# Biases of the experts as three bfloat16 parts, and gather rows and activations stored in the order of the operands' columns

## The chip, the cores and the metric

The kernel runs on one core of a Trainium2 chip. A core has a matrix engine (TensorE, PE in the profile; its weight loads are listed apart as PEld), VectorE (DVE), ScalarE (ACT), GpSimd (POOL), SyncE (SP), which here issues nearly all DMAs, and 16 DMA engines that move data between HBM and the core's memory SBUF. Products land in PSUM, eight banks of 512 float32 columns by 128 partitions. The metric is the device time of one execution in microseconds, as the median of the runs.

## The reference, cut to what matters

One layer for 256 tokens of width 1024 in float32: a mixer (stick-breaking attention and a state-space scan, merged by gates), cross-attention into 256 memory tokens, and a mixture of 32 experts of which each token takes four. The change is in the last of them:

```python
def expert_block(args):
    xb, e = args
    g = jnp.minimum(xb @ w_e_gate[e] + b_e_gate[e], SWIGLU_LIMIT)
    u = jnp.clip(xb @ w_e_up[e] + b_e_up[e], -SWIGLU_LIMIT, SWIGLU_LIMIT)
    act = (u + 1.0) * g * jax.nn.sigmoid(SWIGLU_ALPHA * g)
    return act @ w_e_down[e] + b_e_down[e]
```

Each expert has three weight matrices of 1024 x 1024 float32, 4.194 MB each. All 32 are read once, 402.7 MB.

## The kernel before

*Mixer and cross-attention* (the first 530 us). Projection weights come in pieces of 1 MB and are split into a high and a low part in a shorter format of float32: ScalarE copies the high part (`w_h`, line 96), VectorE subtracts for the low part (`w_l`, line 97), and TensorE makes three products per pair (lines 241 to 244 and 257 to 259). Splits are made three pieces ahead of their products, in four buffers. A scheduler with a cost model orders the instructions of each engine here; where the code switches it off (`manual_schedule`) the order is that of the code.

*Expert stage* (from 530 us). Experts go in groups of four. For a group, `gather` (line 971, products at line 980) collects the tokens of each expert into columns: the rows `xh` and `xl` (high and low part of the normalised tokens) are the stationary operand, a selection matrix is the moving one, 32 products of 256 columns a group. A stationary operand takes every fourth column of a row, since the weights are loaded with the rows `4 p + k` of a matrix in partition `p`. `xl` is made by GpSimd (line 49 within `normal`). Per expert, `bias_of` (line 910) starts the two PSUM banks of gate and up with the biases: a product of a one-hot column with `bgu` in float32, four products of 512 columns into 64 partitions each (line 904). `matmul_cols` (line 947, products at line 951) adds the products of the tokens with the weight chunks; `swiglu` (line 955) forms the activation in `ut`; `act_t` (line 966) transposes it in four steps, again over every fourth column (line 968), into `aT`; then the down products, per pair of experts into the banks `y2`. `scatter` (line 990) adds a pair's result to the tokens.

*Weight chunks.* Each matrix comes in two chunks of 2.097 MB, 192 in all, issued by SyncE in the order of use (line 668; the last expert's down matrix in 16 parts at line 664). A ring of ten slots holds them (tile `mw`), and a slot is issued again when its last product is done. Three slots can be filled during the mixer, the other seven when its buffers are given back at about 504 to 526 us.

*Between the two halves* `overflow` (line 1058 on) handles experts with more than 64 tokens in a loop that may run no time at all. Ahead of and behind that loop all engines meet, and SyncE waits for its loads in flight.

*The end* (from line 1270): the last expert's down products in halves, sums into the tokens, the last normalisation and the output.

Of the kernel before, what the change touches and what calls it, by code (L numbers as in the profile page):

```python
# [17 lines left out]
NB = T // P  # L18
# [100 lines left out]
def body(nc, tc, a, out, dbg=None, stop=99):  # L119
# [7 lines left out]
    with es:  # L127
# [555 lines left out]
        brt = xa.tile([P, NE], F32, name="brt")  # L683
        memh = xa.tile([P, KT, T], F32R, name="memh")
# [39 lines left out]
        nc.gpsimd.tensor_copy(iop, iop_i)  # L724

# [170 lines left out]
        left = cst.tile([P, NB, NE + 4], F32, name="left")  # L896
# [5 lines left out]
        def bias(pg, w, hot4):  # L902
# [7 lines left out]
        def bias_of(pg, w, e):  # L910
            bias(pg, w, lambda r: ident[:, 32 * r + e:32 * r + e + 1].to_broadcast([P, CAP]))
# [50 lines left out]
        def fours(kt):  # L962

            return slice(512 * (kt // 4) + kt % 4, 512 * (kt // 4) + 512, 4)

        def act_t(ut, pa, aT):
# [91 lines left out]
        def overflow():  # L1058
# [17 lines left out]
            hot = mo.tile([P, NE], F32, name="o_hot")  # L1076
            tmp = mo.tile([P, NB, NE], F32, name="o_tmp")
            c2 = mo.tile([P, 2, NB], F32, name="o_col")
            hotp = mo.tile([P, 4], F32, name="o_hotp")
            ovi = mo.tile([P, 1], I32, name="o_i")  # L1080
            shf = mo.tile([P, 2, 15], F32, name="o_shf")
            q32 = mo.tile([P, 4], F32, name="o_q32")
            nc.vector.tensor_scalar(q32, iota[:, 0:4], 32.0, None, op0=ALU.mult)
            with tc.If(nv > 0), tc.For_i(0, nv, 1):
# [5 lines left out]
                nc.vector.tensor_scalar(hotp, q32, ec, iop, op0=ALU.add, op1=ALU.is_equal)  # L1090
# [19 lines left out]
                for w in range(2):  # L1110
                    bias(pg, w, lambda q: hotp[:, q:q + 1].to_broadcast([P, CAP]))
                dst = [[pg[0][0:64], pg[0][64:128]], [pg[1][0:64], pg[1][64:128]], [y2[0][0:64], y2[1][64:128]]]
                for w in range(3):
                    if w == 2:
                        swiglu(pg, gt, ut, st)
                        act_t(ut, pa, aT)
# [45 lines left out]
        for quad in range(NE // 4):  # L1162
# [18 lines left out]
            for pr in range(2):  # L1181
# [13 lines left out]
                for q in range(2):  # L1195
# [48 lines left out]
                    act_t(ut, pa, aT)  # L1244
# [117 lines left out]
```

## Time and profile before

| what | value |
|---|---|
| median of 3 runs | 1497.47 us (1496.65 to 1499.45) |
| profiled execution, own time | 1497.82 us |
| its span, first to last instruction | 1496.1 us, mean granted TensorE clock 0.983 |
| TensorE busy | 1413.6 us (94%) |
| VectorE, ScalarE, GpSimd busy | 635.6 (42%), 416.2 (28%), 16.8 us (1%) |
| read from HBM | 487.33 MB, 326 GB/s over the span |

The profile is of one execution. Busy time of TensorE comes from records whose ends are modelled, so a full engine is not one at its peak; the pace of equal instructions in a row (start to start) says more than their duration. The slices show the span in 40 parts of 37.4 us. A float32 product shows as two records of matmul.

### The profile page before, as it was taken

How to read it: one execution, taken by the hardware profiler on the slowest of the kernel's cores; microseconds unless marked ns; L12 is line 12 of the kernel's file. 1: busy time of each engine (PE TensorE's matmuls, PEld its weight loads, DVE VectorE, ACT ScalarE, POOL GpSimd, SP SyncE). 2: the span in 40 equal slices, each digit the busy share in tenths (PEclk: the TensorE clock that was granted, in tenths of full speed). 3: DMA queues.
4: the chain of work that ended last, by engine and by line, in shares of the span. 5: the costliest groups of instructions: out<-in, count | busy, mean ns of one | idle time of the engine just before them, and what ended most of it. 6: DMA issues, size and time to landing. Idle time of an engine off the chain costs nothing. (4 is left out here: it accounts for less than half of the span.)

```text
span 1496.1 us, 18742 instructions
## 1 busy us (share of the span) xinstructions
PE 1413.6 (94%) x7890; PEld 830.1 (55%) x7890; DVE 635.6 (42%) x1004; ACT 416.2 (28%) x656; POOL 16.8 (1%) x36
## 2 busy tenths in 40 slices
PE   7999998998999999999999999979999999999996
PEld 7988898997899853343343343324334334334333
DVE  7666579998777451621221221221222222222213
ACT  5666678885545310010000000001001001001010
POOL 1000000000000010000000000000000000000001
PEclk9999999999999999999999999999999999999998
DMA  7544445554854689979999999998999999999991
GB/s 243 170 169 169 141 141 184 184 170 144 327 206 141 267 348 428 428 332 402 427 427 427 426 427 426 427 426 373 427 426 427 427 426 427 427 426 427 427 399 48
DMA packets 76133, 489.65 MB, mean 327 GB/s; under 512 B 7379, under 2 KB 11979, under 8 KB 51727
## 3 DMA queue, kind: packets, MB, share of 16 engines
q1 hardware_dynamic: 75772, 488.16, 80.8%
q8 instruction: 63, 1.03, 0.3%
q10 hardware_dynamic: 274, 0.27, 0.1%
q14 instruction: 24, 0.19, 0.0%
HBM read 487.33 MB, written 1.08 MB: 326 GB/s over the span
## 5 line engine op out<-in xcount | busy, mean ns | idle before, releaser
L951 PE MATMUL ps_gu<-mw,xg 128*64 128x512 f32 x2048 | 462.0, 595 | 0.0
L951 PEld LDWEIGHTS ps_gu<-mw,xg 128*64 128x64 f32 x2048 | 147.4, 137 | 269.0 <-issue 262.4
L951 PE MATMUL ps_y<-mw,aT 128*64 128x512 f32 x992 | 222.2, 595 | 0.0
L97 DVE TENSOR_TENSOR w_l<-w_raw,w_h 128x1024 fp32r<-128x1024 f32 x145 | 175.4, 1215 | 88.2 <-ACT w_h L96 87.9
L96 ACT ACTIVATE w_h<-w_raw 128x1024 fp32r<-128x1024 f32 x145 | 152.8, 1057 | 116.6 <-PE ps_t L243 71.8
L241 PE MATMUL ps_t<-hTh,w_h 128*128 128x256 f32 x576 | 164.0, 286 | 2.0 <-DVE gx L331 2.0
L243 PE MATMUL ps_t<-hTl,w_h 128*128 128x256 f32 x576 | 164.0, 285 | 0.0
L244 PE MATMUL ps_t<-hTh,w_l 128*128 128x256 f32 x576 | 162.6, 284 | 0.3 <-DVE w_l L97 0.3
L951 PEld LDWEIGHTS ps_y<-mw,aT 128*64 128x64 f32 x992 | 71.3, 138 | 134.0 <-issue 133.4
L969 ACT ACTIVATE aT<-ps_x 128x512 f32<-128x512 f32 x32 | 19.1, 597 | 342.9 <-PE ps_x L968 342.8
L241 PEld LDWEIGHTS ps_t<-hTh,w_h 128*128 128x128 f32 x576 | 109.9, 191 | 3.3 <-issue 3.1
L243 PEld LDWEIGHTS ps_t<-hTl,w_h 128*128 128x128 f32 x576 | 110.1, 191 | 0.2 <-issue 0.2
L244 PEld LDWEIGHTS ps_t<-hTh,w_l 128*128 128x128 f32 x576 | 109.6, 191 | 0.5 <-DVE w_l L97 0.5
L958 DVE TENSOR_SCALAR ut<-ps_gu 128x512 f32<-128x512 f32 x32 | 22.1, 691 | 199.2 <-PE ps_gu L951 198.9
L904 PE MATMUL ps_gu<-bgu,ident 128*64 128x512 f32 x256 | 71.4, 624 | 24.2 <-DVE gt L956 9.4
L956 DVE TENSOR_SCALAR gt<-ps_gu 128x512 f32<-128x512 f32 x32 | 22.1, 690 | 146.3 <-PE ps_gu L951 146.3
L996 DVE SCALAR_TENSOR_TENSOR y<-ps_y,scl,y 128x512 fp32r<-128x512 f32 x30 | 22.5, 751 | 131.3 <-ACT y L995 128.0
L995 ACT ACTIVATE y<-ps_y,scl 128x512 fp32r<-128x512 f32 x30 | 19.0, 684 | 205.1 <-PE ps_y L951 160.5
L957 ACT ACTIVATE st<-gt 128x512 f32<-128x512 f32 x32 | 20.1, 629 | 179.0 <-DVE gt L956 179.0
L904 PEld LDWEIGHTS ps_gu<-bgu,ident 128*64 128x64 f32 x256 | 17.7, 140 | 66.4 <-issue 26.2
L988 ACT ACTIVATE xg<-ps_x,gb 128x256 f32<-128x256 f32 x32 | 18.1, 564 | 119.4 <-PE ps_x L980 119.4
L1003 DVE TENSOR_TENSOR h<-h,ps_x 128x512 f32<-128x512 f32 x60 | 38.6, 682 | 25.2 <-PE ps_x L1002 25.2
(354 smaller groups left out, 1853.4 us busy)
## 6 DMA issues: line engine op xcount, KB each, us to landing
mw<-in_w_e_gate SPq DMA_DIRECT2D x64, 2048.0 KB, 18.1
mw<-in_w_e_up SPq DMA_DIRECT2D x64, 2048.0 KB, 23.0
mw<-in_w_e_down SPq DMA_DIRECT2D x62, 2048.0 KB, 15.2
w_raw<-in_w_in SPq DMA_DIRECT2D x39, 1024.0 KB, 5.1
w_raw<-in_w_ssd SPq DMA_DIRECT2D x8, 1024.0 KB, 5.2
w_raw<-in_w_sb SPq DMA_DIRECT2D x4, 1024.0 KB, 5.0
csb<-csd SPq DMA_DIRECT2D x8, 512.0 KB, 6.6
w_raw<-in_w_mix_out SPq DMA_DIRECT2D x4, 1024.0 KB, 5.0
```

What stands on the lines that cost most here:

```text
L96: nc.scalar.activation(h, src, AF.Copy)
L97: nc.vector.tensor_tensor(l, src, h.bitcast(F32), op=ALU.subtract)
L241: nc.tensor.matmul(o, wh[:, k, s], xh[:, kt], start=first and j % 2 == 0, stop=False, skip_group_check=True)
L243: nc.tensor.matmul(o, wh[:, k, s], xl[:, kt], start=False, stop=False, skip_group_check=True)
L244: nc.tensor.matmul(o, wl[:, k, s], xh[:, kt], start=False, stop=last, skip_group_check=True)
L904: nc.tensor.matmul(pg[w][64 * i:64 * i + 64], hot4(2 * w + i), bgu, start=True, stop=False, skip_group_check=True)
L951: nc.tensor.matmul(dst[i], lhs(4 * c + k), chunk[:, k, 512 * i:512 * i + 512], start=first and c == 0 and k == 0, stop=c == 1 and k == 3, ...
L956: nc.vector.tensor_scalar(gt, pg[0], LIMIT, None, op0=ALU.min)
L957: nc.scalar.activation(st, gt, AF.Sigmoid, scale=1.702)
L958: nc.vector.tensor_scalar(ut, pg[1], -LIMIT, LIMIT, op0=ALU.max, op1=ALU.min)
L996: nc.vector.scalar_tensor_tensor(yl[r], y2[i][r], scl[r, i:i + 1], yh[r].bitcast(F32), op0=ALU.mult, op1=ALU.subtract)
L1003: nc.vector.tensor_tensor(h2[:, b, s], h2[:, b, s], ps, op=ALU.add)
```

## The change

The biases of gate and up are loaded three times, into partitions 0 to 31, 32 to 63 and 64 to 95 of `bgr`, and turned into three bfloat16 parts in `bgu` (the value, the rest, the rest of the rest) by copies on ScalarE and subtractions on VectorE. A bias product then takes 96 rows: `ident3` has a one in rows e, 32 + e and 64 + e of column e, so one product adds the three parts. There are still four products an expert.

The gather rows `xh` and `xl` are written in the order of columns in which the gather reads them, by reads that step over four (`fours`). The last product of SwiGLU does the same, and goes into `gt` instead of `ut`; the transposes then read 128 columns in a row. The overflow loop gets the same forms, and three small tiles are moved to make room.

```diff
-        bgu = cst.tile([P, 512], F32, name="bgu")
+        bgu = cst.tile([96, 4, 512], BF16, name="bgu")
         for w, n in enumerate(("b_e_gate", "b_e_up")):
-            for i in range(2):
-                q = 32 * (2 * w + i)
-                nc.sync.dma_start(bgu[q:q + 32], a[n][0][:, 512 * i:512 * i + 512])
+            for q in range(3):
+                nc.sync.dma_start(bgr[32 * q:32 * q + 32, 2 * w:2 * w + 2], a[n][0].rearrange("e (i f) -> e i f", i=2))
+        for w in range(2):
+            s = slice(2 * w, 2 * w + 2)
+            nc.scalar.activation(bgu[:, s], bgr[:, s], AF.Copy)
+            for q in (1, 2):
+                for r in [slice(32 * t, 32 * t + 32) for t in range(q, 3)]:
+                    nc.vector.tensor_tensor(bgr[r, s], bgr[r, s], bgu[r, s], op=ALU.subtract)
+                    nc.scalar.activation(bgu[r, s], bgr[r, s], AF.Copy)
+        ident3 = cst.tile([96, 32], BF16, name="ident3")
...
+        def fours(x, sorted=True):
+
+            return x.rearrange("q (k p) -> q k p", k=4) if sorted else x.rearrange("q (p k) -> q k p", k=4)
+
...
-                split(nc, xh[:, b, s], xl[:, b, s], h2[:, b, s], copy=copy, sub=nc.gpsimd)
+                split(nc, fours(xh[:, b, s]), fours(xl[:, b, s]), fours(h2[:, b, s], False), copy=copy, sub=nc.gpsimd)
...
-                nc.tensor.matmul(pg[w][64 * i:64 * i + 64], hot4(2 * w + i), bgu, start=True, stop=False,
-                                 skip_group_check=True)
+                nc.tensor.matmul(pg[w][64 * i:64 * i + 64], hot.to_broadcast([96, CAP]), bgu[:, 2 * w + i], start=True,
+                                 stop=False, skip_group_check=True)
...
-            nc.vector.tensor_tensor(ut, ut, st, op=ALU.mult)
+            nc.vector.tensor_tensor(fours(gt), fours(ut, False), fours(st, False), op=ALU.mult)
...
-                nc.tensor.transpose(pa[:, P * f:P * f + P], ut[:, fours(f)], ident)
+                nc.tensor.transpose(pa[:, P * f:P * f + P], gt[:, P * f:P * f + P], ident)
...
-                            nc.tensor.matmul(o, x[:, b, fours(kt + i)], sel[:, b], start=i == 0 and b == 0 and x is xh,
+                            nc.tensor.matmul(o, x[:, b, P * (kt + i):P * (kt + i) + P], sel[:, b], start=i == 0 and b == 0 and x is xh,
```

Three places of the new order of instructions follow. Line numbers of the changed kernel lie 2 to 20 higher.

On SyncE, among the last weight loads of the mixer (`w_raw`); `brt` is the router's bias:

```order
 L82 DMA w_raw<-in_w_in 128x4x512 x2
 L82 DMA w_raw<-in_w_ssd 128x4x512
-L741 DMA brt<-in_b_router 128x32
+L713 DMA bgr<-in_b_e_gate 32x1024 x3
+L713 DMA bgr<-in_b_e_up 32x1024 x3
+L757 DMA brt<-in_b_router 128x32
 L82 DMA w_raw<-in_w_ssd 128x4x512
 L82 DMA w_raw<-in_w_mix_out 128x4x512 x4
```

The bias loads, four of 64 KB near the start before, are six of 128 KB here and stand ahead of the last `w_ssd` piece.

On ScalarE at the same place (`sq` and `sh` belong to the scan's normalisation, `w_h` are high parts of projection weights):

```order
 L96 ACTIVATE w_h<-w_raw 128x1024
 L581 ACTIVATE sq<-y 128x1024
-L96 ACTIVATE w_h<-w_raw 128x1024 x2
+L716 ACTIVATE bgu<-bgr 96x1024
+L96 ACTIVATE w_h<-w_raw 128x1024
+L716 ACTIVATE bgu<-bgr 96x1024
+L96 ACTIVATE w_h<-w_raw 128x1024
+L720 ACTIVATE bgu<-bgr 32x1024 x2
 L586 ACTIVATE sq<-ps_ms,epst 128x256
+L96 ACTIVATE w_h<-w_raw 128x1024
 L587 ACTIVATE sq<-sq 128x256
+L720 ACTIVATE bgu<-bgr 32x1024 x2
```

Eight copies now stand between the copies of the weights, six on 32 partitions that each wait for a subtraction on VectorE. Those six subtractions stand between `w_l` rows in the same way.

On TensorE, from the first expert to the second; `ps_gu` are the banks of gate and up, before:

```order
L951 MATMUL ps_gu_5758<-mw,xg 64x512 x16
L904 MATMUL ps_gu_5933<-bgu,ident 64x512 x2
L904 MATMUL ps_gu_5934<-bgu,ident 64x512 x2
L951 MATMUL ps_gu_5933<-mw,xg 64x512 x13
L968 MATMUL ps_x<-ident,ut 128x128 x4
L951 MATMUL ps_gu_5933<-mw,xg 64x512 x3
L951 MATMUL ps_gu_5934<-mw,xg 64x512 x16
```

and in the changed kernel:

```order
L971 MATMUL ps_gu_5785<-mw,xg 64x512 x16
L924 LDWEIGHTS ident_4651
L924 MATMUL ps_gu_5960<-bgu,ident_4651 64x512
L924 LDWEIGHTS ident_4651
L924 MATMUL ps_gu_5960<-bgu,ident_4651 64x512
L924 LDWEIGHTS ident_4651
L924 MATMUL ps_gu_5961<-bgu,ident_4651 64x512
L924 LDWEIGHTS ident_4651
L924 MATMUL ps_gu_5961<-bgu,ident_4651 64x512
L971 MATMUL ps_gu_5960<-mw,xg 64x512 x16
L971 MATMUL ps_gu_5961<-mw,xg 64x512
L986 MATMUL ps_x<-ident,gt 128x128 x4
```

The place of the biases is the same; the transposes of the first expert come four products later. Through the rest of the stage the order of products stays within a few of what it was.

## Rows read from the trace of the kernel before

**Rows 1.** The page's 40 slices: granted clock, DMA busy, GB/s.
```profile
PEclk9999999999999999999999999999999999999998
DMA  7544445554854689979999999998999999999991
GB/s 243 170 169 169 141 141 184 184 170 144 327 206 141 267 348 428 428 332 402 427 427 427 426 427 426 427 426 373 427 426 427 427 426 427 427 426 427 427 399 48
```
**Rows 2.** Busy time by stretch: length, engines (instructions), granted clock, DMA share, GB/s.
```profile
1200.00:1300.00 100.00, 94.89 (x438) 38.56 (x436) 21.57 (x39) 7.80 (x13) 0.00 (x0) 0.98 1.01 427
```
**Rows 3.** Chain of waits: shares on the page, two pieces (start, us, what).
```profile
PE 30%; DVE 2%; ACT 0%; issue 0%; DVEq 0%
...
1128.94 4.02 PE ps_x L980 x16
...
1243.44 4.11 PE ps_x L980 x16
```
**Rows 4.** Waits of SyncE's queue: total us, times, longest.
```profile
SPq L668 <- PE ps_gu L951: 538.8, 116, 18.1
```
**Rows 5.** Busy time by stretches of 10 us, columns as in rows 2.
```profile
540.00:550.00 10.00, 10.00 (x44) 5.57 (x42) 3.84 (x8) 1.13 (x2) 0.00 (x0) 1.00 0.48 173
...
660.00:670.00 10.00, 10.00 (x42) 7.06 (x44) 2.12 (x4) 1.69 (x3) 0.00 (x0) 0.83 0.50 213
670.00:680.00 10.00, 10.00 (x46) 4.63 (x44) 1.22 (x3) 0.56 (x1) 0.00 (x0) 1.00 0.51 190
...
1020.00:1030.00 10.00, 10.00 (x45) 4.87 (x47) 1.76 (x4) 1.13 (x2) 0.00 (x0) 1.00 0.64 241
```
**Rows 6.** SyncE in order of time: start, us from first to last issue, count.
```profile
651.94 22.33 SPq L668 DMA_DIRECT2D mw<-in_w_e_down  x3
```
**Rows 7.** Chain of waits, pieces of the group from 1128.94.
```profile
1134.82 2.07 PE ps_x L980 x8
...
1151.28 0.86 PE ps_gu L904 x4
1152.14 3.43 PE ps_gu L951 x16
...
1156.43 0.68 PE ps_x L968 x4
```
**Rows 8.** TensorE in order of time: products with contiguous weights, two forms.
```profile
502.04 0.28 PE L791 MATMUL ps_xo<-pT,xvh 128*128 128x256 f32 x1
502.16 0.29 PE L791 MATMUL ps_xo<-pT,xvl 128*128 128x256 f32 x1
...
516.99 0.81 PE L854 MATMUL ps_tr<-ident,h 128*128 128x128 f32 x6
```
**Rows 9.** In order of time: first gather products, GpSimd's last low part.
```profile
534.78 0.83 PE L980 MATMUL ps_x<-sel,xh 128*128 128x256 f32 x2
...
537.68 1.27 POOL L49 TENSOR_TENSOR xl<-h,xh 128x512 fp32r<-128x512 f32 x1 [0.36 <-DVE xh L48]
```
**Rows 10.** Busy time in the mixer; the page's groups of the split.
```profile
360.00:370.00 10.00, 10.00 (x85) 9.95 (x84) 8.46 (x11) 5.39 (x7) 0.00 (x0) 1.00 0.41 129
370.00:380.00 10.00, 10.00 (x87) 10.00 (x86) 4.41 (x4) 7.04 (x10) 0.00 (x0) 1.00 0.58 206
...
L97 DVE TENSOR_TENSOR w_l<-w_raw,w_h 128x1024 fp32r<-128x1024 f32 x145 | 175.4, 1215 | 88.2 <-ACT w_h L96 87.9
L96 ACT ACTIVATE w_h<-w_raw 128x1024 fp32r<-128x1024 f32 x145 | 152.8, 1057 | 116.6 <-PE ps_t L243 71.8
```
**Rows 11.** The end: busy time by stretch, then two pieces of the chain.
```profile
1456.00:1462.00 6.00, 4.81 (x28) 2.10 (x26) 1.10 (x2) 1.19 (x2) 0.00 (x0) 1.00 0.86 275
1462.00:1468.00 6.00, 4.78 (x18) 2.02 (x20) 0.97 (x2) 0.60 (x1) 0.00 (x0) 0.72 0.02 5
...
1474.43 3.51 PE ps_y L1275 x32
...
1480.21 3.65 PE ps_y L1275 x32
```

More of the change, by code (lines that the diff above doesn't have):

```diff
@@ L683, in body @@
         brt = xa.tile([P, NE], F32, name="brt")
+        bgr = xa.tile([96, 4, 512], F32, name="bgr")
+        ge = xa.tile([P, 3], F32, name="ge")
         memh = xa.tile([P, KT, T], F32R, name="memh")
@@ L705, in body @@
         tap("h1", h1)
[L708 removed]
+        bgu = cst.tile([96, 4, 512], BF16, name="bgu")
         for w, n in enumerate(("b_e_gate", "b_e_up")):
[L710 to L712 removed]
+            for q in range(3):
[8 more added lines that the diff above has]
+        ident3 = cst.tile([96, 32], BF16, name="ident3")
+        nc.vector.tensor_tensor(ident3, ident[:96, 0:32], ident[:96, 32:64], op=ALU.add)
+        nc.vector.tensor_tensor(ident3, ident3, ident[:96, 64:96], op=ALU.add)
         wr = xt_p.tile([P, KT, NE], F32, name="wr")
@@ L724, in body @@
         nc.gpsimd.tensor_copy(iop, iop_i)
+        for t in range(3):
+            nc.vector.tensor_scalar(ge[:, t:t + 1], iop, 32.0 * (t + 1), -32.0, op0=ALU.is_ge, op1=ALU.mult)
+        for t in range(3):
+            nc.vector.tensor_tensor(iop, iop, ge[:, t:t + 1], op=ALU.add)
         rows2 = xt_p.tile([4, 512], F32, name="rows2")
@@ L895, in body @@
         nc.vector.tensor_copy(top[:, :, 0:TOPK], tv[:, :, 0:TOPK])
-        left = cst.tile([P, NB, NE + 4], F32, name="left")
+        left = mt.tile([P, NB, NE + 4], F32, tag="aT", name="left")
         for b in range(NB):
@@ L901, in body, with bias @@
         rows_bcast(g2[1], "ln2_g", 1)
-        def bias(pg, w, hot4):
+        def bias(pg, w, hot):
             for i in range(2):
-                nc.tensor.matmul(pg[w][64 * i:64 * i + 64], hot4(2 * w + i), bgu, start=True, stop=False,
-                                 skip_group_check=True)
+                nc.tensor.matmul(pg[w][64 * i:64 * i + 64], hot.to_broadcast([96, CAP]), bgu[:, 2 * w + i], start=True,
+                                 stop=False, skip_group_check=True)
         def bank_pair():
@@ L910, in bias_of @@
         def bias_of(pg, w, e):
-            bias(pg, w, lambda r: ident[:, 32 * r + e:32 * r + e + 1].to_broadcast([P, CAP]))
+            bias(pg, w, ident3[:, e:e + 1])
         pg0 = bank_pair()
@@ L959, in swiglu, with act_t @@
             nc.vector.scalar_tensor_tensor(ut, ut, 1.0, gt, op0=ALU.add, op1=ALU.mult)
-            nc.vector.tensor_tensor(ut, ut, st, op=ALU.mult)
-        def fours(kt):
-            return slice(512 * (kt // 4) + kt % 4, 512 * (kt // 4) + 512, 4)
-        def act_t(ut, pa, aT):
+            nc.vector.tensor_tensor(fours(gt), fours(ut, False), fours(st, False), op=ALU.mult)
+        def act_t(gt, pa, aT):
             for f in range(4):
-                nc.tensor.transpose(pa[:, P * f:P * f + P], ut[:, fours(f)], ident)
+                nc.tensor.transpose(pa[:, P * f:P * f + P], gt[:, P * f:P * f + P], ident)
             nc.scalar.activation(aT, pa.rearrange("p (f i c) -> p f i c", f=4, i=2), AF.Copy)
@@ L1075, in overflow @@
             pa = x_bank()
-            hot = mo.tile([P, NE], F32, name="o_hot")
-            tmp = mo.tile([P, NB, NE], F32, name="o_tmp")
+            hot = ut[:, 0:NE]
+            tmp = gt[:, 0:NB * NE].rearrange("p (b e) -> p b e", b=NB)
             c2 = mo.tile([P, 2, NB], F32, name="o_col")
-            hotp = mo.tile([P, 4], F32, name="o_hotp")
+            hotp = mo.tile([P, 1], BF16, name="o_hotp")
             ovi = mo.tile([P, 1], I32, name="o_i")
             shf = mo.tile([P, 2, 15], F32, name="o_shf")
-            q32 = mo.tile([P, 4], F32, name="o_q32")
-            nc.vector.tensor_scalar(q32, iota[:, 0:4], 32.0, None, op0=ALU.mult)
             with tc.If(nv > 0), tc.For_i(0, nv, 1):
@@ L1089, in overflow @@
                 nc.vector.tensor_scalar(hot, iota[:, :NE], ec, None, op0=ALU.is_equal)
-                nc.vector.tensor_scalar(hotp, q32, ec, iop, op0=ALU.add, op1=ALU.is_equal)
+                nc.vector.tensor_scalar(hotp, iop, ec, None, op0=ALU.is_equal)
                 for i, v in enumerate((posm, prb)):
@@ L1110, in overflow @@
                 for w in range(2):
-                    bias(pg, w, lambda q: hotp[:, q:q + 1].to_broadcast([P, CAP]))
+                    bias(pg, w, hotp[:96])
                 dst = [[pg[0][0:64], pg[0][64:128]], [pg[1][0:64], pg[1][64:128]], [y2[0][0:64], y2[1][64:128]]]
@@ L1115, in overflow @@
                         swiglu(pg, gt, ut, st)
-                        act_t(ut, pa, aT)
+                        act_t(gt, pa, aT)
                     for c in range(2):
@@ L1243, in body @@
                     aT = mt.tile([P, 4, 2, CAP], F32, tag=("aT", "st")[q], name="aT")
-                    act_t(ut, pa, aT)
+                    act_t(gt, pa, aT)
                     acts.append(aT)
```

## The prediction

> **What bounds the kernel now.** I read the page's slices first. From about 700 us on the line GB/s stands at 426 to 428 in almost every slice, with the line DMA at 9 or 8 [rows 1]; a stretch of 100 us inside it has a DMA share of 1.01 while TensorE is busy 94.89 us of 100 [rows 2]. Two resources are full at once. The chain of waits names only one of them: it runs through TensorE, PE 30% of the span against DVE 2%, and no piece of it is a wait for a weight chunk [rows 3]. The waits of the queue that issues the loads say the same, 538.8 us of waiting for the gate and up products to give a slot back [rows 4]. A reader who stops there takes the expert stage for bound by TensorE alone.
>
> The balance is read from one group of four experts. From the gather at 1128.94 to the next at 1243.44 TensorE took 114.5 us [rows 3]. The weights of four experts are 12 x 4.194 MB = 50.3 MB, and 50.3 MB at 427 GB/s is 117.9 us. So the loads are already slightly the slower of the two, and TensorE runs behind them by what the ten slots hold. Taking TensorE time out therefore moves the end only (a) where DMA stood still for want of a slot and (b) behind the last landing.
>
> For (a) four stretches of 10 us tell where DMA stood still [rows 5]. Against 427 GB/s, 540 to 550 lost (427-173)/427 x 10 = 5.9 us, and nearly another microsecond lies around it, 6.9 in all. 660 to 680 lost 5.0 + 5.6 = 10.6 us. 1020 to 1030 lost 4.4 us. In the second, SyncE's three issues from 651.94 stretch over 22.33 us, so the last went out at 674.27, after a slot that the first products of the second group gave back [rows 6]. For (b), DMA is 0.86 busy from 1456 to 1462 and idle after it, so the last weights landed at 1456 + 0.86 x 6 = 1461.2; TensorE was then behind, and its last down products ended only at 1480.21 + 3.65 = 1483.9 [rows 11].
>
> **The change part by part.**
> *Biases on TensorE.* An expert has four bias products, 512 columns each into 64 PSUM partitions. In the trace each float32 product is two records, and four records cost 0.86 us, so 1.72 us an expert [rows 7]. A record of that form paces at 3.43 / 16 = 0.214 us [rows 7]. The bfloat16 product makes one pass where the record makes two. No 512-column bfloat16 product is in the trace. If the two halves of the array still run side by side, four products cost 2 x 0.214 = 0.43 us; if they run one after the other, 4 x 0.214 = 0.86. I take 0.43, since the float32 pair already runs side by side. Saved: 1.29 us an expert, at least 0.86.
> *Gather rows in order.* The 32 products of a group cost 4.02 us for 16 and 2.07 for each further 8 [rows 3, 7], 8.2 us, 0.26 us each, behind weight loads that step over every fourth column. Products of the same size with contiguous weights start 0.12 us apart [rows 8], so 32 cost 3.8 us. Saved: 4.4 us a group; half of it if something besides the step paces them.
> *Transposes in order.* Four cost 0.68 us [rows 7]; six contiguous ones 0.81 us with the last one's tail in it [rows 8], 0.11 us apart, so four cost 0.44. Saved: 0.24 us an expert, at least nothing.
> Sum per group of four: 4 x 1.29 + 4.4 + 4 x 0.24 = 10.5 us, at least 4 x 0.86 + 2.2 = 5.6. TensorE then needs 104 us (at most 109) where the loads need 117.9. Over 32 experts TensorE gives up 84 us (at least 45), most of which becomes waiting for weights.
> *What comes back of it, (a).* The second standstill ends with the issue at 674.27. Until then TensorE saves five and a half experts' biases, 7.1 us, the two gathers, 6.8 (the first partly covered, below), and four transposes, 1.0: 14.9, of which I count 14 for waits that stay. To keep DMA fed the slot has to come 10.6 us earlier, and 2.4 more because the first standstill shrinks too. 14 covers 13.0 by a hair. I leave 1.5 us of it standing: 9.1 us gained; with the lower bound of 8 us saved, 5.6 of 13.0 stay uncovered and the gain is 5.0.
> At the first standstill the first slot comes back after the gather's fifth and sixth tiles, and these need the low parts from GpSimd, done at 537.68 + 1.27 = 538.95 [rows 9]. That cover keeps the gain to 2.4 us; 0 if GpSimd's reads, now with a step of four, cost it 2 us.
> The stretch at 1020 stays: before it SyncE waits at the branch for all its loads to land, whatever TensorE does.
> Last landing: 1461.2 - 9.1 - 2.4 = 1449.7.
> *(b), the end.* With TensorE waiting for weights, what is late after the last landing is the half of the last down products that uses them. Back from the landing: 22 us before it the last up chunk is in, then 3.4 us of products, 4 of SwiGLU and transposes, 9 of expert 30's down products and start of a sum, then 3.51 us for the first half of expert 31, about 1 of eviction, 1.25 of sums, and 3.65 for the second half [rows 11]. The chain ends 3 to 4 us after the landing, one clock dip included 5. From the end of the down products to the end of the span is 1496.1 - 1483.9 = 12.2 us as before. So landing + 16.
> *The mixer side.* Six subtractions of 1024 columns at 1.215 us are 7.3 us more on VectorE, eight copies at 1.057 are 8.5 more on ScalarE [rows 10], placed around 355 to 380. There VectorE idled 1.5 + 5.6 and ScalarE 4.6 + 3.0 us [rows 10], and TensorE was full. Queued behind a waiting bias copy are the splits of the projection weights, made three splits ahead, about 8 us of products. So most is hidden; without that cover it would be 8.5 us on the path of everything behind. The six bias loads stand before the next projection weights on SyncE, 0.77 MB or 1.8 us at 427 GB/s, where DMA was 0.41 busy. I take +1 us, bounds -2 and +8.
> *Moved reads.* VectorE, ScalarE and GpSimd now read with a step of four values in the split and in SwiGLU's last product. Nothing in the trace shows such a read on these engines; TensorE's weight load, 0.26 against 0.12 us, would double a 0.69 us operation. For 31 experts TensorE has other products to do meanwhile; for the last it costs up to 0.7, held in the range. The Trainium skill (SBUF — State Buffer, Door 1: The DMA port swizzle) says that an access crossing to a new 16-byte line pays a penalty, so that four float32 are as far as one may step for free; the gather's pace agrees, and by that rule the engines that read so now would pay, on a path that waits for weights anyway.
> Sum: 1449.7 + 1 + 16 = 1466.7 span; the profiled execution took 1.7 us beside its span and lay 0.35 above the median, so 1466.7 + 1.35 = **1468 us**.
>
> **The rivals.**
> *The standstill stays:* if the bias halves run one after the other or the gather keeps its pace, the slot at 674 comes too late and only the end is shortened: 1461.2 + 1 + 16 + 1.35 = 1479.5. For it: 14 against 13 leaves no room.
> *TensorE was the whole bound:* the chain read by itself gives 1497.5 - 84 = 1413, or 1452 with the lower saving. Against it: 117.9 us of loads a group at a rate that never leaves 428.
> *Nothing comes of it:* the mixer gives away 8 us, the rest is lost at new waits: 1495 to 1500.
> *The clock, and slower:* TensorE now waits for weights about once a chunk. In the 10 us at 660, after waits around the scatter, its granted clock was 0.83 [rows 5]: a third of them at 1.2 GHz instead of 2.4, 1.7 us lost. A group leaves 117.9 - 104 = 14 us for that, eight such dips. Beyond eight a group TensorE is the bound again; slower than before from about 8 + (29 + 3)/8/1.7 = 10 to 11 a group, for instance 13 a group, 1468 + 5 x 8 x 1.7 = 1536. Against it: a starved TensorE still has 104 of 118 us of dense products, and one that falls behind stops waiting. The Trainium skill (TensorE: Matmul & The Clock Gate, HAM oscillation — how this bites in real kernels) describes a kernel whose waits for DMA between bursts throttle it at every tile; by that rule this one could end at the 1536 too. In the slices of the expert stage the granted clock stands at 9 tenths or more [rows 1], so I give it little.
>
> **How the numbers follow.** Forecast, 1456 to 1474: 0.66. Standstill stays, 1474 to 1486: 0.17. TensorE alone or a faster DMA, below 1456: 0.06. Nothing: 0.05. Slower: 0.06. A measurement tells about 0.2%, 3 us, from no change. Faster 0.89, same 0.05, slower 0.06. The range takes the forecast's and most of the first rival's: 1457 to 1483.
>
> **What would show it.** After: slices of 427 GB/s from 560 on except near 1015; TensorE busy some 84 us less in all, idle before the products on weights and released by their DMA; the chain naming those loads; the last landing near 1450 and the end 16 us behind it; bias products at 0.43 us an expert and gather products 0.12 us apart. Wrong would be a standstill near 665 that stays, a mixer that ends more than 3 us later (the first gather, at 534.78 now [rows 9], marks it), or granted clocks of 0.5 between groups.

## The result, and the profile after

The changed kernel took **1474.38 us** (median of 4, 1472.75 to 1476.22) beside 1497.06 us for the kernel before, a ratio of 0.9846 with the interval 0.9829 to 0.9863. That is 22.7 us less. Forecast were 1468 us and 29 us less: the sign and the main mechanism held, the time lies in the range, and the gain is 6 us short of the forecast. The profiled execution has a span of 1474.5 us and a time of 1476.22, 1.8 us above the median.

The page's slices of the kernel after (granted clock, DMA share, GB/s), to be laid beside [rows 1]:

```profile
PEclk9999999999999999999999999999999999999998
DMA  7545355644675589999999999999999999999994
GB/s 239 172 161 181 122 168 172 200 145 154 237 288 171 203 351 422 427 426 397 428 426 428 428 426 427 429 426 376 429 427 428 428 427 427 427 428 428 427 428 164
```

From the seventeenth slice on, the loads stand at 427. Apart from the last, two slices are lower: 397 near 670 us, where [rows 1] had 332 and 402, and 376 near 1015, where they had 373. The first of the two shrank, the second did not. No slice of the stage but the last shows less than 9 tenths of the clock; stretches at half clock that are shorter than a slice come below.

The same by stretches (columns as in [rows 2]); the first line answers [rows 2], the next five [rows 5], the last the first two of [rows 11]:

```profile
1200.00:1300.00 100.00, 87.90 (x416) 34.54 (x418) 26.20 (x45) 8.46 (x14) 0.00 (x0) 0.98 1.01 427
540.00:550.00 10.00, 10.00 (x50) 4.24 (x48) 4.62 (x10) 1.32 (x3) 0.99 (x1) 0.94 0.46 154
660.00:670.00 10.00, 10.00 (x54) 4.38 (x52) 2.08 (x5) 1.13 (x2) 0.00 (x0) 1.00 0.80 311
670.00:680.00 10.00, 10.00 (x50) 4.29 (x46) 3.18 (x4) 0.63 (x1) 0.00 (x0) 1.00 1.01 429
1020.00:1030.00 10.00, 8.50 (x46) 3.34 (x44) 4.66 (x9) 0.60 (x1) 0.00 (x0) 1.00 0.87 341
1005.00:1030.00 25.00, 22.70 (x116) 9.07 (x114) 7.84 (x13) 1.82 (x3) 0.00 (x0) 1.00 0.86 352
1450.00:1455.00 5.00, 5.00 (x38) 2.52 (x36) 0.00 (x0) 0.00 (x0) 0.00 (x0) 1.00 0.44 138
```

In the 100 us from 1200 on, DMA is as full as before and TensorE has 87.9 us of work instead of 94.9. The standstill near 665 lost (427-311)/427 x 10 = 2.7 us instead of 10.6. The one near 545 did not shrink: 6.4 us in this stretch, 5.9 before. The one near 1020 now begins earlier, so it is read over 25 us: (427-352)/427 x 25 = 4.4 us, as before. The last landing, reckoned from the busy share as in the prediction, is at 1450 + 0.44 x 5 = 1452.2 instead of 1461.2, so 9.0 us earlier. From there to the end of the span are 22.3 us instead of 34.9, so 12.6 us less. The two together are the 21.6 us by which the span fell.

The page's chain of waits and the queue of SyncE (us in total, times, longest), which answer [rows 3] and [rows 4]:

```profile
DMA 19%; PE 12%; DVE 1%; issue 0%; ACT 0%; SPq 0%; DVEq 0%
DMA mw<-in_w_e_down 11%; DMA mw<-in_w_e_up 8%; PE ps_gu L971 7%; PE ps_y L971 3%; PE ps_x L998 1%; PE ps_y L1291 0%; PE ps_x L851 0%; PE ps_acc L1173 0%; PE ps_gu L924 0%; PE ps_x L1019 0%; DVE y L1014 0%; PE ps_x L986 0%; ACT y L1013 0%; DVE h L1021 0%; SPq L668 0%
```

```profile
SPq L668 <- PE ps_gu L971: 252.7, 69, 14.2
SPq L668 <- DMA mw<-in_w_e_down: 161.1, 39, 4.9
SPq L668 <- DMA mw<-in_w_e_gate: 130.9, 31, 5.4
SPq L668 <- DMA mw<-in_w_e_up: 118.1, 30, 5.0
```

The chain now runs through the weight loads, which no piece of it named before. Both chains reach back only to about 1000 us (1007.7 before, 984.3 here), where the engines meet between the two halves, so their shares tell of the last third of the span. SyncE waits for TensorE to give a slot back for 252.7 us instead of 538.8, and for loads that are still under way for 410 us.

The pieces of the chain in one group (start, us, what), beside [rows 7]:

```profile
1110.64 2.17 PE ps_x L998 x16
...
1114.68 1.14 PE ps_x L998 x8
...
1118.54 1.13 PE ps_x L998 x8
...
1129.26 0.22 PE ps_gu L924 x2
...
1133.13 0.58 PE ps_x L986 x4
...
1171.19 39.54 DMA mw<-in_w_e_down
```

Two bias products take 0.22 us, so four take 0.43, as forecast (1.72 before). The 32 gather products take 2.17 + 1.14 + 1.13 = 4.44 us (8.2 before, 3.8 forecast). Four transposes take 0.58 (0.68 before, 0.44 forecast). Half a group further on the chain leaves TensorE and follows a load.

### The profile page after: what moved, and what is told of

The parts are those of the page before. It is cut to its first block, busy times and chain, and to the rows that moved or that the text cites. A ratio compares the mean times of both kernels' runs of the same rounds, so it can differ in the third digit from the quotient of the medians.

```text
span 1474.5 us, 18501 instructions
## 1 busy us (share of the span) xinstructions
PE 1353.5 (92%) x7762; PEld 796.4 (54%) x7762; DVE 657.0 (45%) x1017; ACT 425.5 (29%) x664; POOL 17.8 (1%) x36
## 3 DMA queue, kind: packets, MB, share of 16 engines
HBM read 487.85 MB, written 1.08 MB: 332 GB/s over the span
## 5 line engine op out<-in xcount | busy, mean ns | idle before, releaser
L971 PE MATMUL ps_gu<-mw,xg 128*64 128x512 f32 x2048 | 467.2, 599 | 17.9 <-DMA mw<-in_w_e_up 11.7
L971 PE MATMUL ps_y<-mw,aT 128*64 128x512 f32 x992 | 228.9, 604 | 19.3 <-DMA mw<-in_w_e_down 19.3
L924 PE MATMUL ps_gu<-bgu,ident 96*64 96x512 bf16 x128 | 26.8, 394 | 22.3 <-DVE gt L977 12.4
L1019 PE MATMUL ps_x<-y,selT 128*128 128x512 f32 x60 | 25.0, 458 | 18.1 <-ACT y L1013 11.3
```

Source lines behind the costliest of these rows:

```text
L924: nc.tensor.matmul(pg[w][64 * i:64 * i + 64], hot.to_broadcast([96, CAP]), bgu[:, 2 * w + i], start=True, stop=False, skip_group_check=True)
L971: nc.tensor.matmul(dst[i], lhs(4 * c + k), chunk[:, k, 512 * i:512 * i + 512], start=first and c == 0 and k == 0, stop=c == 1 and k == 3, ...
L1019: nc.tensor.matmul(ps, selT[r, i, P * b:P * b + P], yh[r], start=True, stop=False)
```

## The experiments

My theory: the weight loads bound the expert stage, so TensorE time that is taken out counts only at the standstills of DMA and behind the last landing. The rival: TensorE is the bound, and every microsecond that it loses comes off the end. All ratios are to the kernel before, run beside each kernel (1496.9 to 1497.3 us).

**One half of the change each.** `order_alone` is the kernel before with the ordered storage:

```diff
-                split(nc, xh[:, b, s], xl[:, b, s], h2[:, b, s], copy=copy, sub=nc.gpsimd)
+                split(nc, fours(xh[:, b, s]), fours(xl[:, b, s]), fours(h2[:, b, s], False), copy=copy, sub=nc.gpsimd)
...
-            nc.vector.tensor_tensor(ut, ut, st, op=ALU.mult)
+            nc.vector.tensor_tensor(fours(gt), fours(ut, False), fours(st, False), op=ALU.mult)
...
(gather and transposes read contiguous columns, as in the change)
```

> The kernel before with only the ordered storage of gather rows and activations; float32 biases in one product as before, no splitting of biases in the mixer. Loads are the bound: a group's TensorE time falls by some 4 to 5 us (gather 8.2 to 4.45, transposes 0.68 to 0.58 an expert), the standstill near 665 shrinks by some 4 us, TensorE catches up with the loads and ends 24 to 27 us behind the last landing instead of 34.9: 1481 to 1487, 10 to 16 us faster than before; with the other half alone this adds up to more than 22.7. TensorE is the bound: about 35 us saved of about 75, so 10.5 of the 22.7 us: 1486.5, and the halves add up to 22.7. No mixer cost: the first gather at 534.8, not 535.7.

`bias_alone` is the changed kernel with these lines put back.

> The change without its second half: bfloat16 biases in three parts, but gather rows and activations stored and read as in the kernel before. Loads are the bound: TensorE saves 1.3 us an expert, of which only what comes ahead of the standstill near 665 counts (some 4 of the 7.7 us that the whole change took out of it) and what TensorE is behind the last landing (34.9 us before; it catches up with the loads in any case, so 24 to 26 stay). Less 1 us for the mixer: 1480 to 1485, that is 12 to 17 us faster than before. TensorE is the bound: the gain of 22.7 us splits as the saved TensorE time does, 31 x 1.3 = 40 us of about 75: 12 us, 1485. The two theories are told apart only together with the other half: by the first, the two gains add up to more than 22.7 us, by the second to 22.7. Further: the standstill of 540 to 550 is as wide as in the kernel before if the clock and not GpSimd's stepped writes held it; with GpSimd at fault it shrinks by 1 us or more against the changed kernel.

Measured: `order_alone` 1481.74 us, 0.9892 (0.9877 to 0.9908); `bias_alone` 1480.89 us, 0.9898 (0.9883 to 0.9913). That is 15.1 and 16.0 us faster, 31.1 together, where the whole change gave 22.7. Each gain is known to about 2 us, so the 8 us between are clear of the noise. The gains do not add up, as the theory said and the rival did not. Stretches of `bias_alone`, then of `order_alone`:

```profile
655.00:685.00 30.00, 29.76 (x131) 15.84 (x131) 6.86 (x12) 2.88 (x5) 0.00 (x0) 1.00 0.75 305
...
1455.00:1460.00 5.00, 4.30 (x36) 2.38 (x32) 0.57 (x2) 0.84 (x2) 0.00 (x0) 1.00 0.09 29
```

```profile
655.00:685.00 30.00, 28.06 (x138) 13.07 (x137) 10.00 (x16) 4.15 (x7) 0.00 (x0) 1.00 0.83 345
...
1455.00:1460.00 5.00, 5.00 (x29) 2.01 (x30) 0.00 (x0) 0.00 (x0) 0.00 (x0) 1.00 0.39 127
```

Against 427 GB/s the standstill near 665 costs 8.6 and 5.8 us (10.5 before, 2.8 after, by the same sum). The last landing lies at 1455.5 and 1457.0, so 5.7 and 4.2 us earlier than before. The spans of 1477.4 and 1480.7 us then leave 21.9 and 23.7 us behind the landing. So either half alone brings the 34.9 us of the tail down to about what both bring (22.3): once TensorE needs less than the loads it catches up, and more saving adds nothing there. That common part is why the gains do not add.

**No biases at all.** The changed kernel without the bias products, the first weight product of a bank starting its sum:

```diff
-            bias(pg, w, ident3[:, e:e + 1])
+            return
...
-                                    ..., got[i], c, ks=ks)
+                                    ..., got[i], c, ks=ks, first=True)
```

> The changed kernel with the experts' gate and up biases left out of the expert stage altogether (the first weight product of a bank starts its sum). TensorE has 32 x 0.43 = 14 us less to do. Loads are the bound: 1472 to 1474, at most 2 us faster than the changed kernel (the part of 0.43 x 6 experts ahead of the standstill near 665, and 1 us of the tail). TensorE is the bound: 1474.4 - 13 = 1461.

Measured: 1476.45 us, 0.9866 (0.9851 to 0.9881). Taking a further 14 us of TensorE's work out gave nothing; if anything it took 2 us (within the spread of the runs). The rival's 1461 is excluded, but the time alone is not a clean test: the mean granted clock of the four runs is 0.972 to 0.977, against 0.983 to 0.987 in the changed kernel, so some of the 14 us went into products at half clock. What decides is where TensorE's time went. Its waits ahead of the weight products grew from 17.9 + 19.3 to 23.2 + 37.4 us, while DMA stayed full. The down products on the two pages (their idle time and what ended it are the last column), the changed kernel first, and 400 us of `no_bias`:

```profile
L971 PE MATMUL ps_y<-mw,aT 128*64 128x512 f32 x992 | 228.9, 604 | 19.3 <-DMA mw<-in_w_e_down 19.3
...
L971 PE MATMUL ps_y<-mw,aT 128*64 128x512 f32 x992 | 236.2, 618 | 37.4 <-DMA mw<-in_w_e_down 36.8
...
1030.00:1430.00 400.00, 350.05 (x1608) 127.22 (x1608) 94.24 (x155) 33.28 (x55) 0.00 (x0) 0.98 1.01 428
```

**Half the loads.** Both kernels, with every second chunk of weights left out once the first eleven are on their way:

```diff
                 w, e, c = plan[len(got)]
+                if c == 1 and len(got) > nslots and (w < 2 or e < NE - 1):
+                    got.append(got[-1])
+                    continue
```

> The kernel before with half of the weight loads of the expert stage left out: from the sixth expert pair's turn of the ten slots on, the second chunk of each matrix is not loaded and the first is used twice (the last expert's down matrix is loaded whole). TensorE's work is unchanged, DMA carries half. Theory (before, TensorE ran at its own pace behind full loads and hardly waited for them): 1490 to 1497. If the loads had held it back already: 1480 or less.

> The changed kernel with the same half of the weight loads left out. Theory (TensorE has 60 to 80 us less to do, and the loads alone keep the changed kernel from showing it): 60 to 80 us under the kernel before with half loads, 1415 to 1435, TensorE without waits for weights. Rival (TensorE's own work or the engines that feed it set the time of the changed kernel): about 1470.

Measured: 1477.71 us, 0.9870 (0.9855 to 0.9885), and 1401.16 us, 0.9357 (0.9343 to 0.9372). The busy line of the page, of the kernel before with half loads and of the changed one:

```profile
PE 1424.2 (96%) x7890; PEld 844.7 (57%) x7890; DVE 634.5 (43%) x1004; ACT 415.8 (28%) x656; POOL 16.8 (1%) x36
```

```profile
PE 1346.9 (96%) x7762; PEld 818.7 (58%) x7762; DVE 656.2 (47%) x1017; ACT 425.6 (30%) x664; POOL 17.8 (1%) x36
```

This is the change without its cover. It takes 1477.7 - 1401.2 = 76.5 us out of TensorE, and TensorE's busy time falls by as much, 77.3. With all loads it shows 22.7 of them, and the changed kernel takes 73 us more than with half of them.

Of the two expectations for the kernel before, the time of the second came: it got 19.3 us faster with half the loads, not 0 to 7. But that does not show that the loads had held it back. With half the loads the scheduler also laid the products in another order, in which bias products stand among weight products. The bias products on the two pages, before with all loads and with half:

```profile
L904 PE MATMUL ps_gu<-bgu,ident 128*64 128x512 f32 x256 | 71.4, 624 | 24.2 <-DVE gt L956 9.4
...
L907 PE MATMUL ps_gu<-bgu,ident 128*64 128x512 f32 x256 | 84.2, 619 | 5.2 <-PEq L1087 4.5
```

TensorE's idle time ahead of them, most of it for a bank that VectorE was still reading, fell from 24.2 to 5.2 us, and ahead of the scatter's first products from 19.9 to 12.5. Ahead of the weight products it was 0.0 in both. So in the kernel before TensorE never waited for a weight chunk, and the 19.3 us are not shown to be the loads'; the new order is enough to explain them. The 73 us hold some of the same: ahead of the changed kernel's bias products the idle time is 22.3 us, and 1.5 with half the loads. The 76.5 us between the two half-load kernels stand, since the busy time falls by as much.

**The tail.** Behind the last landing 22.3 us passed, not 16. TensorE in order of time at the end of the changed kernel (start, us, engine, line, count; in brackets its wait and what ended it):

```profile
1428.08 3.23 PE L851 MATMUL ps_x<-rows_a,ident 96*128 96x128 f32 x24
1431.23 7.09 PE L971 MATMUL ps_gu<-mw,xg 128*64 128x512 f32 x32
1441.09 0.63 PE L986 MATMUL ps_x<-ident,gt 128*128 128x128 f32 x4 [2.77 <-DVE gt L982]
...
1458.21 3.67 PE L1291 MATMUL ps_y<-mw,aT 128*64 128x256 f32 x32
```

TensorE has no wait for weights here. The two last up chunks lie ready and are used back to back, because 24 of the 32 transposes that spread the last layer norm's rows stand ahead of them. `early_rows` moves these to the seventh group:

```diff
             e0 = 4 * quad
             fetch(6 * e0 + nslots)
+            if quad == 6:
+                gb = last_rows()
...
-                        gb = last_rows()
```

> The changed kernel with one move: the 32 transposes that spread the last layer norm's gain and bias (4.3 us of TensorE) are issued at the start of the seventh group of experts, where TensorE waits for weights, and not with the last expert. My explanation of the tail (TensorE, not the loads, is late in the last 60 us, because these products, the slots' and the sums' starts all stand there): the last landing stays near 1452, the end comes 4 us earlier, about 1470. Rival (the last landing sets the tail, slowed to some 340 GB/s by the last expert's loads in pieces): no change, 1474.

Measured: 1471.42 us, 0.9821 (0.9808 to 0.9835), 3.0 us less than the changed kernel (the two intervals just overlap; the trace shows where the 3 us come from). The same place there, and its last landing:

```profile
1427.53 3.65 PE L971 MATMUL ps_gu<-mw,xg 128*64 128x512 f32 x16 [0.40 <-DMA mw<-in_w_e_up]
1432.43 3.65 PE L971 MATMUL ps_gu<-mw,xg 128*64 128x512 f32 x16 [1.25 <-DMA mw<-in_w_e_up]
```

```profile
1450.00:1455.00 5.00, 4.30 (x37) 2.63 (x33) 0.84 (x2) 0.84 (x2) 0.00 (x0) 1.00 0.49 158
```

Now TensorE waits for both up chunks, which is what my forecast had assumed. The landing stays (1452.5) and the tail is 1472.2 - 1452.5 = 19.7 us, as the explanation had it and not its rival, a tail set by the last landing alone. `late_acc` also moves the start of the first sums behind the last up products:

```diff
-                    if e == NE - 1:
-                        acc = [start_acc(0)]
                     for w in range(2) if e > 0 else ():
                         for c in range(2):
                             project(w, c)
+                    if e == NE - 1:
+                        acc = [start_acc(0)]
```

> The changed kernel with the layer norm's rows moved to the seventh group and the start of the first block's sums moved behind the last up products, without the repeated bias products. If the repeated products gave nothing: 1470.5, as fill_late_acc, with 6.8 us at half clock at the first gather and 18 us from the last landing to the end. If they gave 1 us or more: 1471.5.

Measured: 1470.43 us, 0.9822 (0.9806 to 0.9838). TensorE there:

```profile
1430.63 3.65 PE L971 MATMUL ps_gu<-mw,xg 128*64 128x512 f32 x16 [1.25 <-DMA mw<-in_w_e_up]
1434.22 1.98 PE L1173 MATMUL ps_acc<-h,ident 128*128 128x512 f32 x4
1436.98 0.66 PE L986 MATMUL ps_x<-ident,gt 128*128 128x128 f32 x4 [0.78 <-DVE gt L982]
1437.56 3.65 PE L971 MATMUL ps_y<-mw,aT 128*64 128x512 f32 x16
```

```profile
1450.00:1455.00 5.00, 4.30 (x34) 2.91 (x34) 2.36 (x6) 0.84 (x2) 0.00 (x0) 1.00 0.15 47
```

The sums' start fills the wait for SwiGLU, 2.68 us before, 0.78 left. The 16 down products behind it take 3.65 us at full clock instead of 5.31, and the tail is 1468.7 - 1450.8 = 17.9 us. Of the 6.3 us that I missed there, the layer norm's rows are 2.6, the sums and the clock 1.8. The 1.8 are read from the two traces; the times do not tell `late_acc` from `early_rows` (0.9822 and 0.9821). The remaining 1.9 are of the size of what the last up chunk brings, though no run tests it: it was in at 1430.6, 20.2 us ahead of the last landing, where I had worked with 22.

**The first gather and the clock.** The standstill near 545 did not shrink. The stretch around the first gather, of `order_alone` and of the changed kernel (the granted clock is the third number from the end):

```profile
525.00:545.00 20.00, 17.53 (x108) 12.17 (x107) 13.76 (x32) 4.98 (x7) 7.05 (x5) 0.91 0.86 358
```

```profile
525.00:545.00 20.00, 16.52 (x95) 11.63 (x94) 13.69 (x31) 4.93 (x7) 6.99 (x5) 0.83 0.80 333
```

Read in stretches of half a microsecond, 0.91 is 3.4 us of the 20 at 1.2 GHz instead of 2.4, and 0.83 is 6.8. The stretch stands at 0.91 in the three kernels with float32 biases (before, `order_alone`, `half_loads_before`). It stands at 0.83 in all nine with bfloat16 ones in which the wait was left as it is, `no_bias` among them. Ahead of the router's first position product TensorE was idle 1.86 us in the kernel before and 2.86 in the changed one: the same wait for the mask, with 0.41 us of bias products before it instead of 1.08. `fill_wait` repeats these products in that wait, in the version with the rows moved:

```diff
-        bias_of(pg0, 0, 0)
+        for _ in range(9):
+            bias_of(pg0, 0, 0)
```

> The changed kernel with the layer norm's rows moved (as in early_rows), and the first two bias products of the first expert repeated nine times, to the same sums, in the wait for the router's mask ahead of the first gather: 16 products more, some 2 us. In the four kernels with bfloat16 biases the clock was at half for 6.8 us at the first gather, in the two with float32 biases for 3.4 us. If the shorter bias products did this by leaving TensorE idle longer ahead of the gather, the stretch at half clock goes back to 3.4 us or away, the first slot comes back 8 us instead of 9.4 after the first gather's start, the standstill near 543 loses 1.4 us and the end comes 1 to 1.5 us earlier than in early_rows: 1470. If it is something else: 6.8 us at half clock and 1471.4 as there.

`fill_late_acc` is the same with the sums moved.

> As fill_wait, and the start of the first block's sums (two products of 512 columns, which each waited 0.8 us for a bank between weight products of the last expert) stands behind the last expert's up products instead, in the wait of 2.7 us for SwiGLU. If TensorE is late at the last weights by what stands ahead of them: the down products run at full clock and up to 2 us come off fill_wait. If the last up chunk's landing sets it (TensorE waited 1.25 us for it in early_rows) and the clock dips all the same: no change.

Measured: 1471.37 us, 0.9830 (0.9816 to 0.9843), and 1470.45 us, 0.9820 (0.9807 to 0.9834). The clock of the 20 us is 0.91 in `fill_wait`. Stretches of `fill_late_acc`, then of `late_acc`, which lacks the filling alone:

```profile
525.00:545.00 20.00, 17.15 (x115) 10.34 (x115) 14.10 (x34) 5.53 (x8) 7.03 (x5) 1.00 0.80 322
530.00:560.00 30.00, 27.40 (x149) 11.51 (x145) 16.62 (x37) 4.50 (x8) 5.42 (x4) 1.00 0.86 348
655.00:685.00 30.00, 30.00 (x149) 13.45 (x150) 6.72 (x11) 4.11 (x7) 0.00 (x0) 1.00 0.89 372
```

```profile
530.00:560.00 30.00, 26.93 (x129) 12.35 (x130) 17.18 (x37) 4.93 (x8) 5.88 (x4) 0.89 0.81 327
655.00:685.00 30.00, 29.89 (x148) 13.52 (x150) 7.38 (x13) 4.11 (x7) 0.00 (x0) 1.00 0.92 382
```

So it is the idle time that lengthens the stretch at half clock, and filling it shortens it or takes it away: two profiles against nine. Up to the last expert the two run the same instructions, so 0.91 against 1.00 is a difference between executions. At full clock the standstill near 545 loses (427-348)/427 x 30 = 5.6 us instead of 7.0, and the one near 665 takes half of that back, 3.9 instead of 3.2. In five profiles without the filling (the changed kernel, `early_rows`, `late_acc`, and `after_again` and `no_split`, which come below) the two standstills together lose 9.8 to 10.2 us by the same sums; with it they lose 9.4 and, in `fill_wait`, 9.1. The time does not tell what is left: 1470.45 against 1470.43 us, and 1471.37 against 1471.42 for `early_rows`. The expectation of 1 to 1.5 us missed; it had left the second standstill out.

The two halves tell the clock from GpSimd here. `order_alone`, in which GpSimd reads with a step and the clock is 0.91, loses (427-343)/427 x 30 = 5.9 us near 545, 1.0 less than the kernel before (6.9). `bias_alone`, in which GpSimd reads in order and the clock is 0.83, loses 7.7 (318 GB/s over the same 30 us), though its gather also keeps its step. So the slower GpSimd is not needed for the standstill that stayed, and where the clock did not fall further it shrank.

**The mixer, and the new waits.** `no_split` leaves the loop of the subtractions out, `rows_only` undoes the activations' half of the ordered storage, `after_again` is the changed kernel:

```diff
(no_split)
-            for q in (1, 2):
-                for r in [slice(32 * t, 32 * t + 32) for t in range(q, 3)]:
-                    nc.vector.tensor_tensor(bgr[r, s], bgr[r, s], bgu[r, s], op=ALU.subtract)
-                    nc.scalar.activation(bgu[r, s], bgr[r, s], AF.Copy)
(rows_only)
-            nc.vector.tensor_tensor(fours(gt), fours(ut, False), fours(st, False), op=ALU.mult)
+            nc.vector.tensor_tensor(ut, ut, st, op=ALU.mult)
...
-                nc.tensor.transpose(pa[:, P * f:P * f + P], gt[:, P * f:P * f + P], ident)
+                nc.tensor.transpose(pa[:, P * f:P * f + P], ut[:, f:512:4], ident)
```

> The changed kernel once more, beside the three others of this series: 1473 to 1476. Its profile is a second sample of the stretch at half clock at the first gather (6.8 us expected) and of the first gather's start, which so far lay anywhere between 531.8 and 536.2 with the new biases.

> The changed kernel without the splitting of the biases in the mixer: the six loads stay, two copies make one bfloat16 part, and the six subtractions and six of the eight copies (13.7 us of VectorE and ScalarE) are left out, so that each part holds the same rounded bias. If the mixer hides the split: no difference, 1473 to 1476. If it costs the 1 us that I forecast or more, as much less, and a first gather by so much earlier than in after_again.

> The changed kernel with the activations as before (SwiGLU's product in place, contiguous; transposes that read every fourth column), gather rows still in order. The loads bound the stage, so the transposes' 0.1 us an expert and the 14.8 us that VectorE waited for the transposes to release gt do not show: 1474 to 1475; the last expert's product takes 0.7 instead of 1.07 us, 0.3 us off the tail. If the new wait for gt costs on the path: 2 us or more faster than the changed kernel.

Measured: `after_again` 1474.22 us, 0.9844 (0.9830 to 0.9858); `no_split` 1474.32, 0.9854 (0.9836 to 0.9872); `rows_only` 1475.48, 0.9843 (0.9827 to 0.9859). None differs from the changed kernel. The split is hidden. The first gather began anywhere from 531.5 to 536.2 us in the nine profiles with bfloat16 biases in the wait as it is, and at 534.8, 535.3 and 537.1 in the three without. A cost of 1 us in the mixer is below this spread, and no mark of it is seen.

## Why the prediction was right, and where it fell short

**The bound.** Right for the changed kernel. Before, TensorE never waited for a weight chunk, so the chain of waits named rightly what came last; the sum of 117.9 us of loads against 114.5 us of TensorE a group [rows 2, 3] told what the chain could not, how soon the loads would take over. The half-load pair shows it directly: 76.5 us saved, 22.7 seen. The rival in which TensorE is the whole bound is dead by `no_bias` and by the two halves. It lies near what the kernel does with half the loads, 1413 there and 1401 measured, but the other order of products has a part in the 1401.

Of the 7.8 us by which the span missed the forecast (1474.5 against 1466.7), 1.5 are the last landing (1452.2 against 1449.7 + 1) and 6.3 the tail. Of the 9.0 us that the landing gained, 7.7 came at the standstill near 665 and none at the other two; the rest stays open.

**TensorE's saving.** Forecast 84 us, measured 76.5. The biases came out as worked out. The gather takes 4.44 us a group instead of 3.8. At full clock its products stood 0.12 us apart in the first group, as [rows 8] had it, but over a group with its starts the pace is 4.44 / 32 = 0.14. The transposes gave 0.1 us an expert instead of 0.24. Behind the standstill near 665 this miss cost nothing, since there the loads set the pace.

**The standstill near 665.** Right that it shrinks and nearly goes; 9.1 us forecast, 7.7 measured. SyncE's third issue, in the changed kernel beside [rows 6]:

```profile
648.98 18.39 SPq L668 DMA_DIRECT2D mw<-in_w_e_down  x3
```

It went out at 667.4 instead of 674.3. Counted from the first gather (535.7 and 534.8) the slot came 131.7 us later instead of 139.5, so TensorE had saved 7.8 us by then. I had counted 14. That is the mis-sized term, and 10.6 - 7.8 = 2.8 us are just what stayed. (In the forecast's lower bound 8 us saved leave 13.0 - 8 = 5.0 us uncovered and gain 5.6, not the other way round; its sum does not use them.) Of the 7.8, 3.9 came between the two gathers, where four experts' biases alone are 5.2. The first gather ran half its way at half clock, and TensorE's waits of 1.33 and 1.49 us for VectorE near 631 had been 0.65 and 0.45. The other 3.9 came behind the second gather's start, about that gather's saving (8.2 - 4.44 = 3.8). The rival in which this standstill stays is dead. How much of it stays does vary: 2.7 to 3.4 us in the five profiles named above, 5.1 in `no_bias` and 6.1 in `rows_only`.

**The standstill near 545.** Wrong: 2.4 us forecast, nothing gained. I had taken GpSimd's low parts for the cover and named 0 as the bound for a slower GpSimd. It did slow down a little, 1.58 us for each of the four subtractions instead of 1.33. But the larger part is the clock, which I had not expected: the first 16 gather products ran at half of it, 0.21 us apart, and at full clock (`fill_late_acc`) 1.4 of the 2.4 us came back at this standstill. Even there little reached the end, since the next standstill took half.

**The one near 1020.** Right: it stayed, 4.4 us as before.

**The tail.** The step that failed. I forecast the end 16 us behind the landing and counted back from it, with TensorE waiting for the last up chunk. The count itself names one clock dip that its sum leaves out: with it 5 + 12.2 = 17.2. I left out of that count the layer norm's 32 transposes, those of the scatter's slots and two waits for a bank, which all stand in the last 60 us. TensorE was late there by its own work, and the end came 22.3 us behind the landing. Two moves bring 17.9.

**The mixer.** Forecast +1 us with bounds -2 and +8; nothing is seen. VectorE was busy 9.88 us of the 10 from 370 on (4.41 in [rows 10]) and TensorE was full all the same, 9.95 us:

```profile
370.00:380.00 10.00, 9.95 (x86) 9.75 (x85) 9.88 (x12) 8.56 (x12) 0.00 (x0) 1.00 0.40 122
```

**Reads with a step.** SwiGLU's last product, unseen before, takes 1.10 us instead of 0.69, 0.4 us against up to 0.7 in the forecast:

```profile
L982 DVE TENSOR_TENSOR gt<-ut,st 128x512 f32<-128x512 f32 x32 | 35.2, 1101 | 3.3
```

The Trainium skill (SBUF — State Buffer, Door 1: The DMA port swizzle) says that each access that crosses to a new 16-byte line pays a penalty. With a step of four float32 every read is on a new line, and VectorE and GpSimd agree here, at 1.6 and 1.2 times the contiguous price. The same passage counts a stride of four float32 as still free; the runs do not bear that out. `rows_only`, which takes this product and the transposes in order back together, is no faster, so the price does not show in the kernel's time.

**The clock rival.** Its time is dead, its mechanism is there twice. TensorE waited for weights, and on average the clock held: 0.99 over 400 us, 1.00 before, with 50 us of idle time in them:

```profile
1030.00:1430.00 400.00, 349.69 (x1640) 130.33 (x1636) 92.03 (x149) 33.19 (x55) 0.00 (x0) 0.99 1.01 428
```

Of the 27 waits for a chunk that are longer than 0.3 us, 25 are 0.4 to 1.4 us, mostly between 3.65 us of products, and the products behind them kept their pace. The other two are longer, and TensorE ran at half clock behind them:

```profile
1082.64 5.96 PE L971 MATMUL ps_gu<-mw,xg 128*64 128x512 f32 x16 [5.60 <-DMA mw<-in_w_e_up]
1210.77 11.91 PE L971 MATMUL ps_y<-mw,aT 128*64 128x512 f32 x48 [4.55 <-DMA mw<-in_w_e_down]
...
1080.00:1085.00 5.00, 2.36 (x6) 0.77 (x8) 0.00 (x0) 0.00 (x0) 0.00 (x0) 0.55 1.01 429
```

The first 16 products took 5.96 us instead of 3.65; the 48 took 11.91, where 48 in the kernel before took 10.47 at full clock. That is 2.3 + 1.4 us in 400, and the rival needed more than eight dips a group. The kernel that the Trainium skill describes (TensorE: Matmul & The Clock Gate, HAM oscillation — how this bites in real kernels) throttles at every tile. The trace agrees behind the two long waits and does not show it behind the short ones.

## What to carry to other kernels

Where DMA is full and an engine too, add both up over one period before trusting the chain of waits: it names the one that comes last, and the other may be a few per cent behind. A saving on the engine then counts only where the loads stand still for want of it and behind the last landing; two kernels with half the loads, with and without the change, show what the saving would be without that cap. Beside a kernel with all loads they say less, since a scheduler may lay the work in another order. Whatever stands ahead of the last data's use on that engine is then the tail: move it to where the engine waits. Doing so here gave 1470.43 us, 4 us off the changed kernel, most of it by the first of the two moves.

## What the runs showed of the hardware beyond that

Less work can lengthen the stretch at half clock. Without the biases the clock of the 20 us at 620 fell to 0.66, against 0.91 in the changed kernel, where TensorE's waits of 2.13 us for the scatter's copy and 3.27 us for SwiGLU's product stand, with no bias products in them (0.43 and 1.49 in the changed kernel). The standstill near 665 then lost 5.1 us (355 GB/s from 655 to 685) instead of 2.8. Of `no_bias`:

```profile
620.00:640.00 20.00, 13.47 (x39) 5.14 (x38) 12.69 (x21) 3.12 (x5) 0.00 (x0) 0.66 1.01 427
```

The gather behind stepping weight loads kept its pace through the clock: 0.234 us a product at 1.2 GHz and at 2.4 in the kernel before. In order it takes 0.214 and 0.12. So the step, and not the clock, was its limit, and a clock that comes back was worth nothing to it.

The last expert's down weights, loaded in pieces, arrive at 341 GB/s from 1440 to 1450, where whole chunks arrive at 427; it was so before too, 333 GB/s from 1450 to 1455.
